# Seven-product FFN blocks: sums of products kept in PSUM half banks that ScalarE fills, with another order of the seven

## The chip, the cores and the metric

The kernel runs on one core of one Trainium2 chip. The metric is the device time of one execution in microseconds (us). The engines are called by the names that the profile uses: PE is TensorE (matrix products, with PEld for its weight loads), ACT is ScalarE, DVE is VectorE, POOL is GpSimd and SP is the queue that starts the large loads. PSUM is the memory that TensorE writes its products to; the kernel uses it as eight banks of 128 partitions by 512 fp32 numbers, and a half bank here is 256 of these columns.

## The reference: two layers with a gated FFN each

The reference is a block of two layers on 512 tokens with 1024 features, all in fp32. Each layer has a mixer (a gated linear recurrence in the first, a dilated attention in the second) and then a feed-forward network (FFN), both with a norm before and after and with scales and shifts from a conditioning vector. The change touches the first half of the FFN only, which is this part of the reference:

```python
def swiglu_ffn(u, w_in, w_out):
    gate, up = jnp.split(u @ w_in, 2, axis=-1)
    return (jax.nn.silu(gate) * up) @ w_out
```

`w_in` is 1024 by 5632 (2816 columns for the gate, 2816 for the up half), and `w_out` is 2816 by 1024.

## The kernel before

**Three products for one.** Each fp32 operand is split into a high part, rounded to the shape that TensorE takes at its fast rate (`F32R`), and a low part, the difference. A product is then three matmuls that add up in PSUM: high by high, high by low and low by high. ScalarE makes the high parts with a copy, VectorE the low parts with a subtraction.

**The FFN's columns.** The 2816 gate and up columns are cut in 22 pieces of 128 (`NF` = 22). In function `ffn`, the first `PLAIN[l]` pairs of pieces (three in the first layer, two in the second) are computed plainly, with 512 tokens as the moving operand. The other pieces, 16 in the first layer and 18 in the second, go through `seven_products`, one piece to a block, so there are 34 blocks.

**A block of seven products.** A block computes gate and up for 128 columns. It treats the work as a 2 by 2 matrix product: weights (gate and up, by the lower and the upper half of the 1024 features) times activations (the two halves of the features, by the two halves of the tokens). Seven products of sums take the place of eight plain ones. The sums of activations (`t1`, `t2`, `T3`, `T4`) are made once per FFN by `token_sums`; `B11`, `B21` and `B22` are plain quarters of the activations. The sums of weights are made in every block: `sum_a` on GpSimd (one 128x512 addition), `sum_b` and `sum_c` on VectorE. The plain quarters of the weights (`R`) are split by `r_hi` and `r_lo`, the sums (`Sm`) by `s_hi` and `s_lo`, each in two cuts. Each of the seven products is one call of `run`: four pieces of the 512 features by three matmuls, twelve matmuls of 128x256, into one half bank.

**Where the products were put together.** In the kernel before, `runs` writes the seven products into four banks: one product alone in its half, the others in pairs. The banks come from the pool's tags `mm` and `a`, `b` by turns, so that a block and the next one use different banks. All additions of products are done outside TensorE, into a scratch tile `W` in SBUF: `sums_1` and `sums_2` on VectorE with a copy of one half bank by ScalarE ahead of each, one addition on GpSimd in `sums_2`, then `sums_3` on VectorE. ScalarE takes the SiLU of the gate (128x512), and `finish` on VectorE multiplies it by the up half into `mid`.

**What sets the order.** The loop over blocks stands in `tc.manual_schedule(engines=ORDERED)`: TensorE, ScalarE, VectorE and GpSimd execute in the order in which the program states their instructions. The framework adds the waits between engines. While TensorE works on block i, the other engines prepare the weights of block i + 1, finish block i - 1, and ScalarE's `r_hi` starts on block i + 2. `st.fill()`, at the end of `s_lo`, starts the load of a later block's weights on SP when a buffer has become free.

**The shift.** `B11` is read from a place 144 columns further on in the activation tiles `uh` and `ul`. The copies that move it there stand at the head of `seven_products`, and in block 0 the run of `B11` comes third for that reason.

**Afterwards** `ffn` takes the eight banks for the outputs of `w_out` (`y0` from tag `mm`, `y1` from tags `a` and `b`), and splits `mid` piece by piece.

Of the kernel before, what the change touches and what calls it, by code (L numbers as in the profile page):

```python
# [158 lines left out]
def block_kernel(tc, x, c, positions, ada_w, ada_b, norm_g, hgrn_w_in, lower, hgrn_norm_g, hgrn_w_out,  # L159
# [8 lines left out]
    with ExitStack() as ctx:  # L168
# [268 lines left out]
        def three(ps, ah, al, bh, bl, start, stop):  # L437
            pe.matmul(ps, ah, bh, start=start, stop=False)  # L438
            pe.matmul(ps, ah, bl, start=False, stop=False)  # L439
            pe.matmul(ps, al, bh, start=False, stop=stop)  # L440
# [327 lines left out]
                    dve.tensor_sub(tl[:, k], t[k], th[:, k].bitcast(F32))  # L768
            return cut

        def seven_products(fs, mid, sgp, spare, th, tl):


            fs = list(fs)
            quarter = lambda a, k: a[:, k * 512:(k + 1) * 512]
            Q4 = lambda a: a.rearrange("p (s n) -> p s n", s=4)
            u_of = lambda r, c: [(uh[:, r * 4 + k, c * 256:c * 256 + 256], ul[:, r * 4 + k, c * 256:c * 256 + 256]) for k in range(4)]
            t_of = lambda i: [(th[:, i, k], tl[:, i, k]) for k in range(4)]
            B21, B22 = u_of(1, 0), u_of(1, 1)

            for copy, t in ((act.copy, uh), (dve.tensor_copy, ul)):
                for a, b in ((112, 256), (0, 112)):
                    copy(t[:, 0:4, a + 144:b + 144], t[:, 0:4, a:b].bitcast(F32))
            B11 = [(uh[:, k, 144:400], ul[:, k, 144:400]) for k in range(4)]
            t1, T3, T4, t2 = (t_of(i) for i in range(4))

            W = shared.rearrange("p a (b n) -> p (a b) n", b=2)
            H2 = lambda a: a.rearrange("p (a n) -> p a n", a=2)
            ring = []
            raw, g_of = {}, {}  # L790

            def places(i):

                p = i % 2
                if len(ring) <= p:
                    ring.append((spare if p == 0 else st.part_tiles(R0), st.part_tiles(R0)))
                return ring[p]

            def r_hi(i):
                if i < len(fs):  # L800
                    raw[i] = st.whole()
                    act.copy(places(i)[0][0][:, 0:1536], raw[i][:, 512:])

            def r_lo(i):
                hi, lo = places(i)[0]
                dve.tensor_sub(lo[:, 0:1536], raw[i][:, 512:], hi[:, 0:1536].bitcast(F32))  # L806

            def sum_a(i):
                r = Q4(raw[i])
                pool.tensor_add(r[:, 2], r[:, 2], r[:, 0])  # L810

            def sum_b(i):
                r = Q4(raw[i])
                dve.tensor_tensor(r[:, 0:2], r[:, 0:3:2], r[:, 1:2].broadcast_to((P, 2, 512)), op=OP.add)  # L814

            def sum_c(i):
                r = Q4(raw[i])
                dve.tensor_add(r[:, 3], r[:, 3], r[:, 1])

            def s_cut(i, k):  # L820
                src = Q4(raw[i])[:, 1:3] if k == 0 else Q4(raw[i])[:, 0:4:3]
                return [Q4(t)[:, 2 * k:2 * k + 2] for t in places(i)[1]] + [src]

            def s_hi(i, k):
                hi, lo, src = s_cut(i, k)
                act.copy(hi, src)  # L826

            def s_lo(i, k):
                hi, lo, src = s_cut(i, k)
                dve.tensor_sub(lo, src, hi.bitcast(F32))  # L830
                if k == 1:
                    raw.pop(i)
                    st.fill()

            def run(ps, w, o, us):
                for kt in range(4):
                    a = slice(o + kt * P, o + (kt + 1) * P)
                    three(ps, w[0][:, a], w[1][:, a], *us[kt], kt == 0, kt == 3)

            def runs(i):  # L840
                R, Sm = places(i)
                b = [bank("mm") for _ in range(4)] if i % 2 == 0 else [bank(t) for t in "abab"]
                g_of[i] = b
                half = lambda n, k: b[n][:, k * 256:k * 256 + 256]
                first = [(half(0, 0), R, 0, B11), (half(3, 1), R, 512, T4), (half(1, 0), R, 1024, B21)]
                for k in (1, 2, 0) if i == 0 else range(3):
                    run(*first[k])
                run(half(1, 1), Sm, 0, t2)
                run(half(2, 1), Sm, 1024, T3)
                run(half(2, 0), Sm, 512, t1)  # L850
                run(half(3, 0), Sm, 1536, B22)

            def sums_1(i):

                dve.tensor_tensor(W[:, 0:5:4], W[:, 2:3].broadcast_to((P, 2, 256)), H2(g_of[i][1]), op=OP.add)

            def sums_2(i):

                dve.tensor_tensor(W[:, 1:6:4], W[:, 4:5].broadcast_to((P, 2, 256)), H2(g_of[i][2]), op=OP.add)
                pool.tensor_add(W[:, 3], W[:, 3], W[:, 5])  # L860

            def sums_3(i):

                if i >= 0:
                    dve.tensor_tensor(W[:, 1:3], W[:, 1:6:4], H2(g_of.pop(i)[3]), op=OP.add)
                    act.activation(W[:, 0:2], W[:, 0:2], AF.Silu)

            def finish(i):
                if i >= 0:
                    dve.scalar_tensor_tensor(H2(mid(fs[i])), W[:, 2:4], -1.0, W[:, 0:2], op0=OP.mult, op1=OP.mult)  # L870

            with tc.manual_schedule(engines=ORDERED):
                r_hi(0)
                r_lo(0)
                sum_a(0)
                sum_b(0)
                sum_c(0)
                for k in range(2):
                    s_hi(0, k)
                    s_lo(0, k)  # L880
                r_hi(1)
                for i in range(len(fs)):
                    more = i + 1 < len(fs)
                    runs(i)
                    sums_3(i - 1)
                    if more:
                        r_lo(i + 1)
                    finish(i - 1)
                    act.copy(W[:, 2], g_of[i][0][:, 0:256])
                    if more:  # L890
                        sum_a(i + 1)
                        sum_b(i + 1)
                        s_hi(i + 1, 0)
                        sum_c(i + 1)
                    sums_1(i)
                    if more:
                        s_lo(i + 1, 0)
                        s_hi(i + 1, 1)
                    act.copy(W[:, 3], g_of[i][2][:, 0:256])
                    if more:  # L900
                        s_lo(i + 1, 1)
                        r_hi(i + 2)
                    sums_2(i)
                sums_3(len(fs) - 1)
                finish(len(fs) - 1)

        def ffn(l, first, close, nxt, side):
            turns.close()
            close()
            with ExitStack() as fx:  # L910
# [4 lines left out]
                with ExitStack() as qx:  # L915
                    sgp = qx.enter_context(tc.tile_pool(name=f"sg{l}", bufs=1, side=side))
                    qp = qx.enter_context(tc.tile_pool(name=f"quarters{l}", bufs=1, side=bass.opposite_side(side)))
                    spare = [qp.tile([P, 3 * 512 + R0 - k * R0], F32R, name=f"spare{l}{k}")[:, R0 - k * R0:] for k in range(2)]
                    qp.tile([P, 112], F32, name=f"pad_q{l}")
                    th = qp.tile([P, 4, 4, 256], F32R, name=f"th{l}")  # L920
                    tl = qp.tile([P, 4, 4, 256], F32R, name=f"tl{l}")
                    for j in range(PLAIN[l]):
                        if j == 0:
                            pss = first
                        else:
                            pss = []
                            for i in range(2):
                                w = st.take()
                                pss += [block(*w, k * P, 256) for k in range(2)]
                        sg = [fresh(sgp, [P, S], "sg", 2) for _ in range(2)]  # L930
                        for k in range(2):
                            act.activation(sg[k], pss[k], AF.Silu)
                        if j == 0:
                            cut = token_sums(th, tl, midt[:, NF - 8:])
                        for k in range(2):
                            dve.tensor_mul(mid(2 * j + k), pss[2 + k], sg[k])
                        if j == 0:
                            cut()
                            fixed.close()
                    seven_products(range(2 * PLAIN[l], NF), mid, sgp, spare, th, tl)  # L940
                fl.drain()
                roll = fx.enter_context(tc.tile_pool(name=f"roll{l}", bufs=1, side=bass.opposite_side(side)))
                y0 = [bank("mm") for _ in range(NT)]
# [969 lines left out]
```

## Time and profile before

| | |
|---|---|
| median of 3 runs | 1515.11 us (1514.31 to 1516.73) |
| span of the profiled execution | 1511.0 us |
| time of the profiled execution itself | not recorded beside its span |
| PE busy | 1492.8 us, 99% of the span |
| DVE, ACT, POOL busy | 70%, 48%, 16% of the span |
| mean granted clock of TensorE | 0.997 |
| blocks of seven products, first FFN | from 381.63 to 535.35 us of the span |
| blocks of seven products, second FFN | from 1211.69 to 1384.61 us of the span |

The span runs from the first to the last instruction; the time of a run has what lies around the span as well. A row of the timeline gives the start in us from the span's start, the duration in us, the engine, the line of the kernel, the operation, what it writes and reads, the shape, and in brackets how long the engine had been idle and what ended the wait. Matmuls overlap, so the spacing of their starts says how fast they go, and not their duration. In the rows of the seven products, `hiq`, `loq` and `spare` are split weights, `uh` and `ul` the activations, `th` and `tl` the sums of activations, `shared` is the scratch tile `W`. A row of the windows gives, for a stretch, its length and the busy time and count of each engine, then the granted clock, the share of the DMA engines and GB/s. A row of the waits gives who waited for whom, the us in total, the times, and the longest.

### The profile page before, as it was taken

How to read it: one execution, taken by the hardware profiler on the slowest of the kernel's cores; microseconds unless marked ns; L12 is line 12 of the kernel's file. 1: busy time of each engine (PE TensorE's matmuls, PEld its weight loads, DVE VectorE, ACT ScalarE, POOL GpSimd, SP SyncE). 2: the span in 40 equal slices, each digit the busy share in tenths (PEclk: the TensorE clock that was granted, in tenths of full speed). 3: DMA queues.
4: the chain of work that ended last, by engine and by line, in shares of the span. 5: the costliest groups of instructions: out<-in, count | busy, mean ns of one | idle time of the engine just before them, and what ended most of it. 6: DMA issues, size and time to landing. Idle time of an engine off the chain costs nothing. (4 is left out here: it accounts for less than half of the span.)

```text
span 1511.0 us, 23542 instructions
## 1 busy us (share of the span) xinstructions
PE 1492.8 (99%) x9231; PEld 1308.2 (87%) x9231; DVE 1063.6 (70%) x1841; ACT 720.3 (48%) x1219; POOL 234.4 (16%) x208
## 2 busy tenths in 40 slices
PE   8999999999999999999999999999999999999998
PEld 6777888898999988888987888988888899999886
DVE  4587867486888896476667766686466978888633
ACT  4433443363454533375545666346655644544231
POOL 1011211031222211140001110011002212221100
PEclk9999999999999999999999999999999999999999
DMA  9654444125333366423166540365213333334521
GB/s 309 183 166 138 156 140 167 56 85 167 113 107 106 105 208 220 155 100 123 57 195 169 150 129 29 113 195 140 84 46 123 98 100 112 109 105 154 209 96 56
DMA packets 206943, 199.14 MB, mean 132 GB/s; under 512 B 6840, under 2 KB 164720, under 8 KB 206576
## 3 DMA queue, kind: packets, MB, share of 16 engines
q1 hardware_dynamic: 203856, 190.87, 40.6%
q10 hardware_dynamic: 1952, 6.65, 1.2%
q8 instruction: 72, 1.18, 0.3%
q0 software_dynamic: 1024, 0.13, 0.2%
q14 instruction: 39, 0.32, 0.1%
HBM read 192.31 MB, written 5.31 MB: 131 GB/s over the span
## 5 line engine op out<-in xcount | busy, mean ns | idle before, releaser
L89 DVE TENSOR_TENSOR lo<-raw,hi 128x2048 fp32r<-128x2048 f32 x68 | 158.8, 2337 | 91.7 <-ACT hi L88 91.7
L88 ACT CAST hi<-raw 128x2048 fp32r<-128x2048 f32 x68 | 129.7, 1908 | 190.3 <-DMA raw<-in_ffn_w_out_dram 55.2
L438 PE MATMUL ps_mm<-apart,hi 128*128 128x512 f32 x384 | 151.4, 394 | 0.0
L439 PE MATMUL ps_mm<-apart,hi 128*128 128x512 f32 x384 | 151.1, 394 | 0.0
L440 PE MATMUL ps_mm<-apart,lo 128*128 128x512 f32 x384 | 150.7, 394 | 0.1
L438 PE MATMUL ps_mm<-uh,hi 128*128 128x512 f32 (+1 forms) x400 | 146.3, 366 | 0.0
L439 PE MATMUL ps_mm<-ul,hi 128*128 128x512 f32 (+1 forms) x400 | 144.3, 361 | 1.0 <-DVE ul L538 1.0
L440 PE MATMUL ps_mm<-uh,lo 128*128 128x512 f32 (+1 forms) x400 | 144.6, 361 | 0.0
L826 ACT CAST hiq<-raw 128x1024 fp32r<-128x1024 f32 x68 | 68.1, 1048 | 64.2 <-DVE raw L814 63.4
L438 PE MATMUL ps_mm<-hi,oh 128*128 128x512 f32 x240 | 94.0, 392 | 0.0
L439 PE MATMUL ps_mm<-lo,oh 128*128 128x512 f32 x240 | 93.4, 389 | 0.0
L438 PEld LDWEIGHTS ps_mm<-uh,hi 128*128 128x128 f32 x400 | 75.5, 189 | 19.7 <-issue 8.4
L439 PEld LDWEIGHTS ps_mm<-ul,hi 128*128 128x128 f32 x400 | 75.6, 189 | 12.1 <-DVE ul L538 1.4
L440 PEld LDWEIGHTS ps_mm<-uh,lo 128*128 128x128 f32 x400 | 75.5, 189 | 11.4
L440 PEld LDWEIGHTS ps_mm<-apart,lo 128*128 128x128 f32 x384 | 72.2, 188 | 15.0 <-DVE lo L89 0.5
L439 PEld LDWEIGHTS ps_mm<-apart,hi 128*128 128x128 f32 x384 | 72.2, 188 | 14.2
L438 PEld LDWEIGHTS ps_mm<-apart,hi 128*128 128x128 f32 x384 | 72.2, 188 | 14.0
L830 DVE TENSOR_TENSOR loq<-raw,hiq 128x1024 fp32r<-128x1024 f32 x68 | 80.0, 1218 | 0.4 <-ACT hiq L826 0.4
L259 DVE SCALAR_TENSOR_TENSOR shared<-raw,cond,shared 128x512 f32<-128x512 f32 x98 | 73.3, 748 | 9.8 <-DMA raw<-in_ada_w_dram 8.8
L261 POOL PARTITION_ALL_REDUCE shared<-shared x14 | 45.9, 3278 | 200.5 <-DVE shared L259 200.5
L810 POOL TENSOR_TENSOR raw<-raw 128x512 f32<-128x512 f32 x34 | 54.7, 1609 | 101.1 <-DVE loq L806 46.3
L440 PE MATMUL ps_mm<-hi,ol 128*128 128x512 f32 x176 | 68.5, 389 | 0.0
(450 smaller groups left out, 4355.2 us busy)
## 6 DMA issues: line engine op xcount, KB each, us to landing
raw<-in_ada_w_dram SPq DMA_DIRECT2D x40, 1024.0 KB, 5.1
raw<-in_ffn_w_in_dram SPq DMA_DIRECT2D x136, 256.0 KB, 3.5
raw<-in_attn_w_in_dram SPq DMA_DIRECT2D x48, 512.0 KB, 5.1
raw<-in_ffn_w_out_dram SPq DMA_DIRECT2D x22, 1024.0 KB, 4.8
raw<-in_hgrn_w_in_dram SPq DMA_DIRECT2D x12, 1024.0 KB, 5.4
raw<-in_attn_w_in_dram SPq DMA_DIRECT2D x12, 1024.0 KB, 4.9
raw<-in_ffn_w_in_dram SPq DMA_DIRECT2D x10, 1024.0 KB, 5.0
first<-in_ada_w_dram SPq DMA_DIRECT2D x14, 512.0 KB, 7.5
```

Of the source, the lines that this page charges most:

```text
L88: self.nc.scalar.copy(hi, t)
L89: self.nc.vector.tensor_sub(lo, t, hi.bitcast(F32))
L259: dve.scalar_tensor_tensor(a, r[:, k], sc, a, op0=OP.mult, op1=OP.add)
L261: pool.partition_all_reduce(a, a, P, bass.bass_isa.ReduceOp.add)
L438: pe.matmul(ps, ah, bh, start=start, stop=False)
L439: pe.matmul(ps, ah, bl, start=False, stop=False)
L440: pe.matmul(ps, al, bh, start=False, stop=stop)
L810: pool.tensor_add(r[:, 2], r[:, 2], r[:, 0])
L826: act.copy(hi, src)
L830: dve.tensor_sub(lo, src, hi.bitcast(F32))
```

## The change

Sums of products are no longer put together by VectorE and GpSimd. They are built in PSUM: ScalarE copies a finished partial sum into another half bank, and the next product is added onto it by matmuls that don't begin afresh (`start=False`).

- The class `Sums` names the half banks of a block: `first` and `both` in two banks taken once per FFN (`fresh_1`, `fresh_x`), `pair` (a bank with halves `u2` and `u4`) and `last` in three banks of the plain part (`pss`, now `seeded`). Blocks alternate between two halves, and between two banks for `pair`.
- The order of the seven is now B11, T3, t2, B21, t1, T4, B22. Before it was B11, T4, B21, t2, T3, t1, B22, with T4, B21, B11 ahead in block 0.
- B11 starts `first`, and T3 starts `both`. ScalarE copies `first` to `u2`; t2 is added onto `u2`, and B21 onto `first`. ScalarE copies `u2` to `last`; t1 is added onto `last`, and T4 onto `u2`. ScalarE copies `last` to `u4`; B22 is added onto `last`. A fourth copy takes `both` to the scratch tile.
- The SiLU is taken in two halves, from `first` and from `last` directly. One VectorE addition (`tail_b`) adds the copy of `both` to the two halves of `pair`, and `tail_c` multiplies, as `finish` did, now ahead of `r_lo` in VectorE's order.
- `sum_a`, `sum_b` and the casts of the next block's weights have other places in the order, both `s_hi` now ahead of the copy to `u4`; the shift copies stand in block 0, after its third copy, and block 0's B11 reads the unshifted quarter.

```diff
+            fresh_1, fresh_x = bank("a"), bank("b")
+            class Sums:
+                def __init__(self, i):
+                    p = i % 2
+                    self.first = half(fresh_1, p)
+                    self.both = half(fresh_x, p)
+                    self.pair = seeded[p]
+                    self.u2, self.u4 = half(self.pair, 0), half(self.pair, 1)
+                    self.last = half(seeded[2], p)
...
+            def run(ps, w, o, us, begin):
                 for kt in range(4):
                     a = slice(o + kt * P, o + (kt + 1) * P)
-                    three(ps, w[0][:, a], w[1][:, a], *us[kt], kt == 0, kt == 3)
+                    for m, (x, y) in enumerate(((0, 0), (0, 1), (1, 0))):
+                        pe.matmul(ps, w[x][:, a], us[kt][y], start=begin and kt + m == 0, stop=kt == 3 and m == 2,
+                                  skip_group_check=True)
...
+            def tail_a(i, s):
+                    act.activation(W[:, 1], s.last, AF.Silu)
+            def tail_b(i, s):
+                    dve.tensor_tensor(W[:, 2:4], W[:, 4 + i % 2:5 + i % 2].broadcast_to((P, 2, 256)), H2(s.pair), op=OP.add)
...
                 for i in range(len(fs)):
                     more = i + 1 < len(fs)
-                    runs(i)
-                    sums_3(i - 1)
+                    R, Sm = places(i)
+                    s = Sums(i)
+                    run(s.first, R, 0, B11[i > 0], True)
+                    run(s.both, Sm, 1024, T3, True)
+                    tail_a(i - 1, before)
+                    tail_b(i - 1, before)
+                    act.copy(s.u2, s.first)
+                    tail_c(i - 1)
+                    run(s.u2, Sm, 0, t2, False)
+                    run(s.first, R, 1024, B21, False)
                     if more:
                         r_lo(i + 1)
-                    finish(i - 1)
-                    act.copy(W[:, 2], g_of[i][0][:, 0:256])
+                        sum_a(i + 1)
+                    act.copy(W[:, 4 + i % 2], s.both)
+                    act.copy(s.last, s.u2)
+                    if i == 0:
+                        shift()
+                    run(s.last, Sm, 512, t1, False)
+                    run(s.u2, R, 512, T4, False)
                     if more:
-                        sum_a(i + 1)
                         sum_b(i + 1)
                         s_hi(i + 1, 0)
                         sum_c(i + 1)
-                    sums_1(i)
-                    if more:
+                        s_hi(i + 1, 1)
                         s_lo(i + 1, 0)
-                        s_hi(i + 1, 1)
-                    act.copy(W[:, 3], g_of[i][2][:, 0:256])
+                    act.copy(s.u4, s.last)
+                    act.activation(W[:, 0], s.first, AF.Silu)
+                    run(s.last, Sm, 1536, B22, False)
                     if more:
                         s_lo(i + 1, 1)
                         r_hi(i + 2)
-                    sums_2(i)
+                    before = s
```

More of the change, by code (lines that the diff above doesn't have):

```diff
@@ L769, in token_sums, with seven_products @@
             return cut
-        def seven_products(fs, mid, sgp, spare, th, tl):
+        def seven_products(fs, mid, seeded, spare, th, tl):
             fs = list(fs)
-            quarter = lambda a, k: a[:, k * 512:(k + 1) * 512]
             Q4 = lambda a: a.rearrange("p (s n) -> p s n", s=4)
@@ L779, in seven_products, with shift @@
             B21, B22 = u_of(1, 0), u_of(1, 1)
-            for copy, t in ((act.copy, uh), (dve.tensor_copy, ul)):
+            B11 = [u_of(0, 0), [(uh[:, k, 144:400], ul[:, k, 144:400]) for k in range(4)]]
+            def shift():
                 for a, b in ((112, 256), (0, 112)):
-                    copy(t[:, 0:4, a + 144:b + 144], t[:, 0:4, a:b].bitcast(F32))
-            B11 = [(uh[:, k, 144:400], ul[:, k, 144:400]) for k in range(4)]
+                    for copy, t in ((act.copy, uh), (dve.tensor_copy, ul)):
+                        copy(t[:, 0:4, a + 144:b + 144], t[:, 0:4, a:b].bitcast(F32))
             t1, T3, T4, t2 = (t_of(i) for i in range(4))
@@ L788, in seven_products @@
             H2 = lambda a: a.rearrange("p (a n) -> p a n", a=2)
+            half = lambda b, k: b[:, k * 256:k * 256 + 256]
             ring = []
-            raw, g_of = {}, {}
+            raw = {}
+            fresh_1, fresh_x = bank("a"), bank("b")
[7 more added lines that the diff above has]
+                    self.last = half(seeded[2], p)
             def places(i):
@@ L833, in s_lo, with tail_c @@
                     st.fill()
-            def run(ps, w, o, us):
+            def run(ps, w, o, us, begin):
                 for kt in range(4):
                     a = slice(o + kt * P, o + (kt + 1) * P)
-                    three(ps, w[0][:, a], w[1][:, a], *us[kt], kt == 0, kt == 3)
[L840 to L862, printed above, removed]
-                if i >= 0:
-                    dve.tensor_tensor(W[:, 1:3], W[:, 1:6:4], H2(g_of.pop(i)[3]), op=OP.add)
-                    act.activation(W[:, 0:2], W[:, 0:2], AF.Silu)
-            def finish(i):
+                    for m, (x, y) in enumerate(((0, 0), (0, 1), (1, 0))):
+                        pe.matmul(ps, w[x][:, a], us[kt][y], start=begin and kt + m == 0, stop=kt == 3 and m == 2,
+                                  skip_group_check=True)
+            def tail_a(i, s):
+                if i >= 0:
+                    act.activation(W[:, 1], s.last, AF.Silu)
+            def tail_b(i, s):
+                if i >= 0:
+                    dve.tensor_tensor(W[:, 2:4], W[:, 4 + i % 2:5 + i % 2].broadcast_to((P, 2, 256)), H2(s.pair), op=OP.add)
+            def tail_c(i):
                 if i >= 0:
@@ L881, in seven_products @@
                 r_hi(1)
+                before = None
                 for i in range(len(fs)):
                     more = i + 1 < len(fs)
-                    runs(i)
-                    sums_3(i - 1)
+                    R, Sm = places(i)
[8 more added lines that the diff above has]
+                    run(s.first, R, 1024, B21, False)
                     if more:
                         r_lo(i + 1)
-                    finish(i - 1)
-                    act.copy(W[:, 2], g_of[i][0][:, 0:256])
+                        sum_a(i + 1)
[5 more added lines that the diff above has]
+                    run(s.u2, R, 512, T4, False)
                     if more:
-                        sum_a(i + 1)
                         sum_b(i + 1)
@@ L902, in seven_products @@
                         r_hi(i + 2)
-                    sums_2(i)
-                sums_3(len(fs) - 1)
-                finish(len(fs) - 1)
+                    before = s
+                tail_a(len(fs) - 1, before)
+                tail_b(len(fs) - 1, before)
+                tail_c(len(fs) - 1)
         def ffn(l, first, close, nxt, side):
@@ L939, in ffn @@
                             fixed.close()
-                    seven_products(range(2 * PLAIN[l], NF), mid, sgp, spare, th, tl)
+                    seven_products(range(2 * PLAIN[l], NF), mid, pss, spare, th, tl)
                 fl.drain()
```

## The prediction

> **What bounds the kernel now.** I read the page's busy table first, then the waits of TensorE, then the two stretches that the change touches as windows, then one block there in order of time.
>
> ```profile
> span 1511.0 us, 23542 instructions
> PE 1492.8 (99%) x9231; PEld 1308.2 (87%) x9231; DVE 1063.6 (70%) x1841; ACT 720.3 (48%) x1219; POOL 234.4 (16%) x208
> ```
>
> TensorE is busy for 99% of the span; no other engine is above 70%. A busy TensorE row may hide a slow one, so the waits come next: eleven rows, the longest and the shortest shown.
>
> ```profile
> PE ps_mm L1140 <- DVE late L1135: 2.0, 3, 1.3
> ...
> PE ps_b L1831 <- ACT h L1809: 1.7, 2, 1.3
> ...
> PE ps_a L1755 <- DVE h L1811: 0.2, 1, 0.2
> ```
>
> None of the eleven is in the seven products; they stand in the mixers and norms. The two windows are blocks 2 to 15 of the first FFN (14 blocks) and all 18 of the second:
>
> ```profile
> core 0: us, PE busy (x) PEld busy (x) DVE busy (x) ACT busy (x) POOL busy (x), PEclk, DMA share, GB/s
> 400.95:535.35 134.40, 134.40 (x1178) 134.40 (x1177) 115.36 (x128) 65.11 (x84) 31.51 (x28) 1.00 0.40 118
> 1211.69:1384.61 172.92, 172.92 (x1513) 172.92 (x1512) 144.41 (x158) 82.64 (x106) 38.52 (x33) 1.00 0.38 111
> ```
>
> Busy equals length in both: TensorE never pauses, at full clock (1.00). 134.40/14 = 9.60 us a block, 84 matmuls. So time here goes up by whatever pause is added, and goes down only if a matmul gets shorter or goes away. One block, first matmuls of B11, T4, the last of t1, the first of B22, the first of the next block:
>
> ```profile
> 448.95 0.28 PE L438 MATMUL ps_a<-uh,hiq 128*128 128x256 f32 x1
> ...
> 450.37 0.29 PE L438 MATMUL ps_b<-th,hiq 128*128 128x256 f32 x1
> ...
> 457.08 0.28 PE L440 MATMUL ps_a<-th,loq 128*128 128x256 f32 x1
> 457.19 0.28 PE L438 MATMUL ps_b<-uh,hiq 128*128 128x256 f32 x1
> ...
> 458.55 0.28 PE L438 MATMUL ps_mm<-uh,spare 128*128 128x256 f32 x1
> ```
>
> A run of twelve matmuls takes 458.55-457.19 = 1.36 us (0.113 each); B11's takes 1.42. What the other engines do beside it:
>
> ```profile
> 450.31 0.63 ACT L866 ACTIVATE shared<-shared 128x512 f32<-128x512 f32 x1 [0.77 <-DVE shared L865]
> 454.93 2.00 ACT L826 CAST hiq<-raw 128x1024 fp32r<-128x1024 f32 x2 [1.97 <-DVE raw L814]
> 457.39 0.37 ACT L899 COPY shared<-ps_a 128x256 f32<-128x256 f32 x1 [0.46 <-PE ps_a L440]
> 457.66 1.48 ACT L802 CAST hiq<-raw 128x1536 fp32r<-128x1536 f32 x1
> ...
> 450.14 1.75 DVE L806 TENSOR_TENSOR spare<-raw,spare 128x1536 fp32r<-128x1536 f32 x1
> 451.81 0.68 DVE L870 SCALAR_TENSOR_TENSOR mid<-shared 128x512 f32<-128x512 f32 x1
> 453.67 1.23 DVE L814 TENSOR_TENSOR raw<-raw 128x1024 f32<-128x1024 f32 x1 [1.18 <-POOL raw L810]
> 455.54 0.68 DVE L855 TENSOR_TENSOR shared<-shared,ps_b 128x512 f32<-128x512 f32 x1
> 456.14 2.35 DVE L830 TENSOR_TENSOR loq<-raw,hiq 128x1024 fp32r<-128x1024 f32 x2
> 458.41 0.68 DVE L859 TENSOR_TENSOR shared<-shared,ps_a 128x512 f32<-128x512 f32 x1
> 459.19 0.69 DVE L865 TENSOR_TENSOR shared<-shared,ps_b 128x512 f32<-128x512 f32 x1
> ...
> 452.02 1.61 POOL L810 TENSOR_TENSOR raw<-raw 128x512 f32<-128x512 f32 x1 [1.78 <-DVE spare L806]
> 459.17 0.74 POOL L860 TENSOR_TENSOR shared<-shared 128x256 f32<-128x256 f32 x1 [5.53 <-DVE shared L859]
> ```
>
> **The change, part by part.** *Matmuls.* 34 blocks of 84 matmuls of 128x256, before and after: 0.
>
> *Removed sums.* Per block VectorE loses L855, L859 and L865 (3 x 0.68) and gains one 128x512 sum; GpSimd loses L860 (0.74). TensorE waits for none of them, so this is worth 0. ScalarE loses a 128x512 SiLU and two copies and gains four copies and two half SiLUs, some 1.0 us more on an engine busy 65.11 of 134.40: 0 by load, and what counts is when each copy runs.
>
> *The copies between runs.* A partial sum now goes on only after a copy. From a run's last matmul to the first of a run that needs the copy: the matmul's own 0.28 (457.08 to 457.36), 0.03 to the copy (457.39), the copy 0.37 (L899, the same size out of PSUM), then TensorE's restart, which this place shows:
>
> ```profile
> 824.13 0.58 ACT L1809 COPY h<-ps_a 128x512 f32<-128x512 f32 x1
> 824.76 0.30 PEld L1831 LDWEIGHTS ps_b<-h,V 128*128 128x128 f32 x2 [1.77 <-ACT h L1809]
> 824.76 0.49 PE L1831 MATMUL ps_b<-h,V 128*128 128x128 f32 x2 [1.34 <-ACT h L1809]
> 825.09 0.39 PE L1830 MATMUL ps_b<-h,V 128*128 128x128 f32 x2
> ...
> 825.31 0.39 PE L1831 MATMUL ps_b<-h,V 128*128 128x128 f32 x2
> ```
>
> 0.05 after the copy ended (824.71), and the first pair takes 0.33 against 0.22 for the next: 0.11 more. Sum 0.28+0.03+0.37+0.05+0.11 = 0.84, less the 0.113 that passes anyway: 0.73 us that must lie under another run. A run is 1.36.
> - first to u2: T3's run lies between, 0.63 spare: 0. Its cover gone, 0.73.
> - u2 to last: B21's run lies between: 0.
> - last to u4: T4's run lies between t1 and B22, but T4 accumulates in the other half of the very bank that this copy writes. In the built program the copy waits for 36 matmuls more than the copy into last did: twelve each of B21, t1 and T4. It starts only after T4, the run before B22, and B22 adds onto what the copy read and waits for it. Nothing is left to cover it: 0.73 a block.
>
> The Trainium skill, "PSUM — Partial Sum Buffer", section "PSUM bank collisions raise a hardware error", says that TensorE and ScalarE must not touch one bank and quadrant of partitions together, even at different columns, so waits go by bank and not by address. By that rule the price is the 0.73 above; by address alone the halves are disjoint, and the price would be 0. No run here shows a collision; the wait in the built program agrees with the rule.
>
> The unknown is a copy that writes PSUM; no row does. From below, the slope alone, half of what L1809 takes beyond L899: (0.58-0.37) = 0.21, so 0.57 a block. From above, 0.63, the 128x512 L866: 0.99. I take 0.37, the same size from the same memory. Ends: 34 x 0.57 = 19 us and 34 x 0.99 = 34 us.
>
> *What stands ahead of the u4 copy on ScalarE.* The two L826 casts, which wait for a chain from the block's start: SiLU of the block before (0.20 after its end, some 0.40), L870's product 0.68, L806 1.75, L810 1.61, L814 1.23, the casts 2.00 = 7.87, and five hand-overs of 0.03 to 0.13: about 8.2. T4 ends at 1.42 + 5 x 1.36 = 8.22, and the copy may start 0.20 later: 8.42. The chain is just inside: 0. Behind the waiting copy stand the SiLU of first and the L802 cast; 0.37+0.27+1.48 later they end at about 10.5, when the next block's first SiLU is due (10.33+0.20): 0.
>
> *T3 from fifth to second.* The last weight cast it needs (L830's pair, ended 458.49) was ready before the block began (458.55); now needed 1.42 after a start that itself comes 0.73 later: 0.
>
> *The shift copies*, from before block 0 into it:
>
> ```profile
> 379.67 1.26 ACT L783 CAST uh<-uh 128x576 fp32r<-128x576 f32 x2
> 382.02 1.85 DVE L783 CAST ul<-ul 128x576 fp32r<-128x576 f32 x2
> ```
>
> They were hidden under T4 and B21; now they stand ahead of block 1's weight casts and of block 0's u4 copy, which waits for T4 anyway. 0, at most 1.3 us in each FFN if the casts slip.
>
> *Queues and ends.* The DMA issues keep their order and SP passes nothing new; GpSimd has one instruction fewer in its chain. After the last block the output products use the same banks: the ninth matmul needs the last VectorE sum, which can run under B22. 0, at most 1 us each.
>
> **Sum.** 34 x 0.73 = 24.8 us. The record has the profiled execution as its span, 1511.0, which is 4.1 below the median of 1515.1; the 4.1 around it stays. Span 1535.8, time 1539.9.
>
> **Rivals.**
> 1. *Not slower.* The u4 copy gets under T4's run, as the other two get under theirs. It decides if the copy's start does not depend on T4's end: then 0.63 is spare and TensorE stays gapless. For it: disjoint halves and ScalarE idle half the time. Against: the count in the wait. Price 0: 1515 us, or 1512 if B11's slower 0.06 and T4's 0.02 a block went too (34 x 0.08 = 2.7).
> 2. *All three copies show.* If a copy into PSUM took over 0.37+0.63 = 1.0 us, the first two would stick out as well; at 1.1 us each: 34 x (0.73+0.73+0.10+0.10) = 56, 1571 us. Short of that, one only as long as 0.63 gives 1549. Against: no ScalarE row of this size is above 0.63.
> 3. *A slower clock after each pause.*
>
> ```profile
> 1174.51 1.09 PE L519 MATMUL ps_b<-ident,xn 128*128 128x128 f32 x8 [0.58 <-DVE xn L513]
> ...
> 1175.87 0.28 PE L438 MATMUL ps_mm<-uh,hi 128*128 128x256 f32 x1
> 1175.98 0.28 PE L439 MATMUL ps_mm<-ul,hi 128*128 128x256 f32 x1
> ```
>
> After a pause of 0.58 matmuls come 0.11 apart, so the trace speaks against it. If the run after each pause went at half rate: 34 x 1.36 = 46 more, 1586 us. The Trainium skill, "TensorE: Matmul & The Clock Gate", section "A second HAM failure mode: psum-queue depth-cycling", tells of short idles between groups of matmuls that cost clock; the clock of 1.00 in the windows shows none so far.
>
> **How the numbers follow.** Forecast 0.86; rival 1 0.06; rival 2 with its shorter form 0.06; rival 3 0.02. The forecast's own ends are 1515 + 19 = 1534 and 1515 + 34 = 1549; that range, 1534 to 1549, holds the forecast nearly whole and leaves out about 0.15. A change below 0.2%, 3 us, can't be told from none. Slower 0.94 (forecast, 2, 3), same 0.05 and faster 0.01 (rival 1).
>
> **What would show it.** In the waits of TensorE a new row of 34 pauses, released by ScalarE's copy into u4, of 0.5 to 0.7 each; each pause between T4 and B22 and nowhere else; blocks of 10.3 us; TensorE's busy time unchanged, its share near 97%; copies into PSUM of about 0.37; no waits behind the copies into u2 and last. Wrong would be: no such row; pauses at t2 or t1; matmuls over 0.113 apart after a pause; or a copy that starts later than 0.2 after T4, held by the casts.

## The result, and the profile after

The changed kernel takes 1537.32 us in the median (1535.01 to 1538.07), the kernel before 1514.96 us beside it. The ratio is 1.0144, with a 95% interval of 1.0129 to 1.0158: slower by 1.4%, some 22 us. The execution that was profiled took 1537.67 us itself, with a span of 1536.0.

The page's first lines and busy table of the changed kernel:

```profile
span 1536.0 us, 23393 instructions
PE 1503.7 (98%) x9231; PEld 1312.8 (85%) x9231; DVE 1024.2 (67%) x1773; ACT 745.8 (49%) x1321; POOL 199.4 (13%) x174
```

The same 9231 matmuls, VectorE and GpSimd relieved, and a span 25.0 us longer than the 1511.0 of before. The busy table alone would mislead: TensorE is still at 98%, and its busy time even rose by 10.9 us. The waits of TensorE tell more (who waited for whom, us in total, times, longest):

```profile
PE ps_mm L856 <- ACT ps_mm L909: 15.2, 34, 0.4
PE ps_mm L1153 <- DVE cols L1183: 2.4, 1, 2.4
```

The top row is new: 34 waits, one for each block, all released by L909, ScalarE's copy into `u4`. There is no row for the copies into `u2` (L890) and `last` (L898). One such wait in order of time: the end of T4's run and the start of B22 on TensorE, then the first matmul of the block that these belong to and of the block after it.

```profile
464.53 0.28 PE L856 MATMUL ps_mm<-tl,hiq 128*128 128x256 f32 x1
464.65 0.28 PE L856 MATMUL ps_mm<-th,loq 128*128 128x256 f32 x1
465.37 0.39 PE L856 MATMUL ps_mm<-uh,hiq 128*128 128x256 f32 x1 [0.45 <-ACT ps_mm L909]
465.59 0.28 PE L856 MATMUL ps_mm<-ul,hiq 128*128 128x256 f32 x1
...
456.52 0.28 PE L856 MATMUL ps_a<-uh,hiq 128*128 128x256 f32 x1
...
466.85 0.28 PE L856 MATMUL ps_a<-uh,spare 128*128 128x256 f32 x1
```

The starts of T4's last and B22's first matmul are 465.37-464.65 = 0.72 apart instead of 0.113, and the next follows after 0.22 instead of 0.113. Together 0.71 us more, and the two spacings behind them add 0.01; the block takes 466.85-456.52 = 10.33 instead of 9.60, 0.73 more. Only 0.45 of it is shown as idle, because T4's last matmul counts as busy for its 0.28 and the late first matmul for 0.39. That is why the waits sum to 15.2 us only, and busy time rose though no matmul was added. What ScalarE and GpSimd did in the same block:

```profile
462.30 2.00 ACT L843 CAST hiq<-raw 128x1024 fp32r<-128x1024 f32 x2 [1.01 <-DVE raw L831]
464.96 0.36 ACT L909 COPY ps_mm<-ps_mm 128x256 f32<-128x256 f32 x1 [0.66 <-PE ps_mm L856]
465.23 0.39 ACT L910 ACTIVATE shared<-ps_a 128x256 f32<-128x256 f32 x1
...
459.72 1.29 POOL L827 TENSOR_TENSOR raw<-raw 128x512 f32<-128x512 f32 x1 [9.04 <-DVE spare L823]
```

The copy starts 0.03 after T4's last matmul has ended (464.65+0.28 = 464.93) and B22 starts 0.05 after the copy. ScalarE had been idle for 0.66 before it, waiting for TensorE, so the casts did not set its start. TensorE and ScalarE wait for each other, one behind the other, once a block.

### The profile page after: what moved, and what is told of

Same layout as the page of the kernel before. It is cut to its first block, busy times and chain, and to the rows that moved or that the text cites. A ratio compares the mean times of both kernels' runs of the same rounds, so it can differ in the third digit from the quotient of the medians.

```text
span 1536.0 us, 23393 instructions
## 1 busy us (share of the span) xinstructions
PE 1503.7 (98%) x9231; PEld 1312.8 (85%) x9231; DVE 1024.2 (67%) x1773; ACT 745.8 (49%) x1321; POOL 199.4 (13%) x174
## 5 line engine op out<-in xcount | busy, mean ns | idle before, releaser
L856 PE MATMUL ps_mm<-th,hiq 128*128 128x256 f32 x340 | 93.9, 276 | 0.0
L856 PE MATMUL ps_mm<-tl,hiq 128*128 128x256 f32 x340 | 93.9, 276 | 0.0
L856 PE MATMUL ps_mm<-th,loq 128*128 128x256 f32 x340 | 93.9, 276 | 0.0
L827 POOL TENSOR_TENSOR raw<-raw 128x512 f32<-128x512 f32 x34 | 44.9, 1319 | 329.2 <-DVE spare L823 145.8
```

The costliest lines, as they stand in the source:

```text
L856: pe.matmul(ps, w[x][:, a], us[kt][y], start=begin and kt + m == 0, stop=kt == 3 and m == 2, skip_group_check=True)
```

## The experiments

The theory: the two halves `u2` and `u4` lie in one bank, T4 accumulates into the one, so the program makes the copy into the other wait for T4's end, and nothing covers it. The rivals: a copy into PSUM costs its pause wherever it stands; or the casts ahead of it on ScalarE set its time.

**u4 in a bank of its own.** The changed kernel leaves the fourth plain bank empty; `u4` goes there.

```diff
-self.u2, self.u4 = half(self.pair, 0), half(self.pair, 1)
+self.u2, self.u4 = half(self.pair, 0), half(seeded[3], p)
...
-dve.tensor_tensor(W[:, 2:4], W[:, 4 + i % 2:5 + i % 2].broadcast_to((P, 2, 256)), H2(s.pair), op=OP.add)
+dve.tensor_tensor(W[:, 2], W[:, 4 + i % 2], s.u2, op=OP.add)
+dve.tensor_tensor(W[:, 3], W[:, 4 + i % 2], s.u4, op=OP.add)
```

> Edit: u4 goes from the second half of u2's bank into the fourth plain bank, which the changed kernel leaves empty; VectorE's closing sum becomes two sums of 128x256. The copy into u4 then waits for t1's last matmul instead of T4's, and T4's run (1.36 us) can lie over it; it stays behind both weight casts on ScalarE. Theory (the shared bank makes the pause): the 34 pauses of 0.4 to 0.5 us of TensorE behind the copy L909 go, blocks are 9.60 us again instead of 10.33, the span falls by 25 us to about 1511, the time to about 1513 to 1515. It is tight: in the changed kernel the casts ended 0.66 before T4's end plus 0.3, so the copy can end only just before T4 does; a rest of up to 0.2 a block (7 us) is allowed. Rival (a copy that writes PSUM costs TensorE its pause wherever it stands): blocks stay at 10.33, about 1537. Rival (the casts ahead of the copy set its start, not the bank): the pauses shrink by no more than the 0.66 that the casts have to spare, and what is left is released by the copy again.

Measured: 1511.8 us, 0.9991 of the kernel before (0.9979 to 1.0003). The whole loss is gone. T4's last and B22's first matmul on TensorE, then the casts and the copy into `u4` (here L910) on ScalarE:

```profile
458.34 0.28 PE L856 MATMUL ps_mm<-th,loq 128*128 128x256 f32 x1
458.45 0.28 PE L856 MATMUL ps_mm<-uh,hiq 128*128 128x256 f32 x1
...
455.99 2.00 ACT L843 CAST hiq<-raw 128x1024 fp32r<-128x1024 f32 x2 [1.01 <-DVE raw L831]
457.89 0.37 ACT L910 COPY ps_mm<-ps_mm 128x256 f32<-128x256 f32 x1
```

B22 follows T4 after 0.11. The copy now runs while T4's matmuls are under way, and ends at 458.26, 0.19 before B22 starts. It still stands behind the casts, and starts when they let it: this cover is thin, but it holds. The copies are the same, as many and as long; only the bank differs, and VectorE's closing sum, which is in two parts. That refutes the rival by which a copy into PSUM costs a pause wherever it stands.

**The same, with the copy ahead of the second cast.**

```diff
                         sum_c(i + 1)
+                    act.copy(s.u4, s.last)
+                    if more:
                         s_hi(i + 1, 1)
                         s_lo(i + 1, 0)
-                    act.copy(s.u4, s.last)
```

> Edit: as the kernel with u4 in a bank of its own, and the copy into u4 stands ahead of the second of the two weight casts on ScalarE (1.0 us earlier in the queue). Theory (the shared bank makes the pause): TensorE runs without a pause from block to block as in the kernel before, 9.60 us a block, 84 matmuls at 0.113; time 1513 to 1515, same as before, and not faster, since the matmuls are the same. If the kernel with u4 apart alone still shows pauses, they were the casts' and are gone here. Rival (a copy that writes PSUM costs a pause wherever it stands): about 1537.

Measured: 1513.37 us, 0.9994 (0.9984 to 1.0004), the same as before. No wait of TensorE stands behind any of these copies. In the block from 450.30 on the copy ends at 457.74 and B22 starts at 458.55, 0.81 later instead of 0.19. With 0.6 us more of cover (not the 1.0 of the expectation) nothing more is gained: the thin cover of the kernel above cost nothing. The relief of VectorE and GpSimd gains nothing clear of noise either: with the pause gone, a block takes the 9.60 us of its 84 matmuls again.

**T3's run between T4 and B22.** `u4` stays in the shared bank. This lays T3's run over the copy into `u4` and takes it away from the copy into `u2`. The copy of T3's product moves behind the next block's first SiLU (in `tail_a`).

```diff
                     act.activation(W[:, 1], s.last, AF.Silu)
+                    act.copy(W[:, 4 + i % 2], s.both)
...
                     run(s.first, R, 0, B11[i > 0], True)
-                    run(s.both, Sm, 1024, T3, True)
...
-                    act.copy(W[:, 4 + i % 2], s.both)
                     act.copy(s.last, s.u2)
...
                     act.copy(s.u4, s.last)
                     act.activation(W[:, 0], s.first, AF.Silu)
+                    run(s.both, Sm, 1024, T3, True)
                     run(s.last, Sm, 1536, B22, False)
```

> Edit: u4 stays in u2's bank; T3's run moves from the second place of the block to the place between T4 and B22, and the copy of its sum for the closing sums goes behind the next block's first SiLU. Now T3's run (1.36 us) lies between T4, whose end the copy into u4 waits for, and B22, which needs the copy; but nothing lies any more between B11 and t2, which needs the copy into u2. Theory (a pause is what lacks of 0.84 us under a run): no pause at B22, a new one of the same size at t2 (0.73 a block, 0.4 to 0.5 of it idle), blocks 10.33 us, about 1537 again. Rival (B22 waits for something else than the copy's end, or T3's place itself costs): the pause at B22 stays as well, blocks above 11 us, 1560.

Measured: 1548.86 us (ratio 1.0243, 1.0221 to 1.0265), 12 above the expectation. The waits of TensorE in this kernel:

```profile
PE ps_mm L856 <- ACT ps_mm L890: 16.9, 34, 1.3
```

The pause moved to t2, which waits for the copy into `u2` (L890), as expected. But blocks took 10.61 us (B11 to B11, 436.16 to 446.77). The rest stands before B22: T3's last and B22's first two matmuls, then ScalarE's casts and the copy into `u4` (here L908).

```profile
444.99 0.28 PE L856 MATMUL ps_b<-th,loq 128*128 128x256 f32 x1
445.25 0.38 PE L856 MATMUL ps_mm<-uh,hiq 128*128 128x256 f32 x1
445.48 0.28 PE L856 MATMUL ps_mm<-ul,hiq 128*128 128x256 f32 x1
...
442.93 2.00 ACT L843 CAST hiq<-raw 128x1024 fp32r<-128x1024 f32 x2 [2.66 <-DVE raw L831]
444.83 0.37 ACT L908 COPY ps_mm<-ps_mm 128x256 f32<-128x256 f32 x1
```

B22 is 0.15 late and its first matmul 0.11 longer. T4 had ended at 443.91, but the casts came 1.0 us later in the block than in the changed kernel, since the moved copy of T3's product holds up VectorE's closing sum and all that stands behind it. T4 itself ends 0.66 earlier in the block than in the changed kernel, as T3's 1.36 no longer stands ahead of it and the pause at t2, some 0.70, does. So the 0.66 that ScalarE had to spare was more than used up, and the copy waited 0.9 for the casts. That was a side effect of this edit, not foreseen in the expectation.

**The same, with the copy ahead of the second cast**, by the same edit as above.

> Edit: as the kernel with T3's run between T4 and B22, and the copy into u4 stands ahead of the second of the two weight casts on ScalarE. That kernel took 10.61 us a block and not the 10.33 expected of it: beside the pause at t2 (0.45 idle) its trace shows B22 starting 0.15 late with a first matmul 0.11 longer, 0.05 after a copy that began only when the casts were done (444.83 against T4's end at about 443.9). Theory (T3 covers the copy, and the casts ahead of it in the queue used up the cover): that late start at B22 goes, 0.24 to 0.28 a block, 34 x 0.24 to 0.28 = 8 to 10 us less than the 1548.9 of that kernel, 1539 to 1541, and the pause at t2 stays as it is. Rival (the late start at B22 is T3's or the bank's own): it stays near 1549.

Measured: 1549.92 us (1.0229, 1.0213 to 1.0245). T3's last and B22's first matmul, and the copy into `u4` (here L906):

```profile
446.16 0.28 PE L856 MATMUL ps_b<-th,loq 128*128 128x256 f32 x1
446.28 0.28 PE L856 MATMUL ps_mm<-uh,hiq 128*128 128x256 f32 x1
...
445.07 0.36 ACT L906 COPY ps_mm<-ps_mm 128x256 f32<-128x256 f32 x1
```

The late start is gone: the copy ends at 445.43, 0.85 before B22. The time didn't fall: in its number this is the rival's outcome, but not for the rival's reason. The matmuls on t1, t2 and T4 took longer here. One form of them (the columns are busy us, mean ns of one, idle before), first in this kernel, then in the one with `u4` apart:

```profile
L856 PE MATMUL ps_mm<-tl,hiq 128*128 128x256 f32 x340 | 95.4, 281 | 0.0
```

```profile
L856 PE MATMUL ps_mm<-tl,hiq 128*128 128x256 f32 x340 | 93.9, 276 | 0.0
```

Runs of twelve matmuls took 1.41 us instead of 1.36, in all blocks but three. The block is 9.60, plus 0.73 for the pause at t2, plus 6 x 0.05 for the six runs that were quick before: 10.63, and 10.62 was seen. So what was gained at B22 was lost to pace; the pace is taken up below.

**The copy into u4 twice.**

```diff
                     act.copy(s.u4, s.last)
+                    act.copy(s.u4, s.last)
```

> Edit: the copy into u4 is issued twice, one behind the other; all else as changed. Theory (the whole copy lies open, nothing covers any part of it): each pause grows by one copy, 0.36 less whatever of it the two overlap; 34 x 0.27 to 0.36 = 9 to 12 us more, about 1547 to 1549. Rival (a part of the copy is hidden, and the pause is set by something else that ends at the same time, such as the weight casts of the next block): less than 5 us more, 1537 to 1542.

Measured: 1552.12 us (1.0254, 1.0238 to 1.0269), 14.8 above the changed kernel. Both copies on ScalarE, and B22's first matmul:

```profile
443.69 0.36 ACT L909 COPY ps_mm<-ps_mm 128x256 f32<-128x256 f32 x1 [0.67 <-PE ps_mm L856]
444.08 0.36 ACT L910 COPY ps_mm<-ps_mm 128x256 f32<-128x256 f32 x1
...
444.49 0.39 PE L856 MATMUL ps_mm<-uh,hiq 128*128 128x256 f32 x1 [0.83 <-ACT ps_mm L910]
```

The second copy starts 0.39 after the first: the two didn't overlap, and 0.03 lies between them beside their 0.36. The block took 10.77 instead of 10.33. 0.39 is the copy, 0.04 is B22's run at a longer pace (1.52 against 1.48), and 0.01 is B11's. The copy lies open in full; the rival with a hidden part falls. My upper end, 0.36 a block, was too low by the hand-over between the two and by that pace.

**The copy into u4 cut to 32 columns.** 224 of the 256 columns of that sum are left out.

```diff
-                    act.copy(s.u4, s.last)
+                    act.copy(s.u4[:, 0:32], s.last[:, 0:32])
```

> Edit: of u4 the copy carries only the first 32 of its 256 columns; 224 columns of that sum are left out, the rest of the output's work is as changed. Theory (the whole hand-over lies open: last matmul's tail 0.28, copy, restart): the pause shrinks by the length that the copy loses. L1809 and L899 of before (0.58 for 512 columns, 0.37 for 256) give 0.21 for 256 columns, so 224 columns are worth 0.18 a block; 34 x 0.18 = 6 us, about 1531, and 0.55 of the 0.73 stays, for it is the tail, the restart and the fixed part of a copy. Rival (the pause is mostly the moving of the data): it all but goes, 34 x 0.6 = 20 us, about 1517. Rival (the pause is set by something beside the copy): nothing changes, 1537.

Measured: 1530.81 us (1.0105, 1.0091 to 1.0119), 6.5 below the changed kernel. The answers on the copy's line, in this kernel and in the changed one (ns least/median/most, first and last start):

```profile
L909 ACT COPY ps_mm<-ps_mm x34: 170/170/170, 392.4 to 1402.4; 128x32 f32<-128x32 f32 x34
```

```profile
L909 ACT COPY ps_mm<-ps_mm x34: 357/357/357, 392.7 to 1407.7; 128x256 f32<-128x256 f32 x34
```

An eighth of the columns takes 170 of 357 ns, so 0.187 us less, x 34 = 6.4 us. The blocks took 10.15 instead of 10.33: 0.01 of the gain is lost again in B22's run (1.49 against 1.48). The pause keeps 0.55 of its 0.73, as expected: the matmul's tail, the fixed part of the copy, the two hand-overs and the restart. Making the copy smaller can't save this order.

**An aside: where B11 reads.** B11's run takes 1.42 us before and after the change, every other run 1.36. Here `u4` is apart with its early copy, and B11 reads the unshifted place in every block; the shift copies go.

```diff
-                    run(s.first, R, 0, B11[i > 0], True)
+                    run(s.first, R, 0, B11[0], True)
...
-                    if i == 0:
-                        shift()
```

> An aside. Edit: as the kernel with u4 in a bank of its own and its copy ahead of the second cast, and B11's run reads its products' inputs from where B11 was stored first, in every block, so that the eight copies that shift it (four to an FFN) go. Question: B11's run takes 1.42 us and the two matmuls after it 0.02 more where every other run takes 1.36. If the shifted place of the inputs makes it: 34 x 0.06 to 0.08 = 2.0 to 2.7 us less than the kernel with its copy early (1513.4), about 1511. If it is the place in the block (the start of the weights' DMA or the end of the block's casts): the same 1513.4, and B11 still 1.42. If the first place is the worse one: slower by an amount that no row bounds.

Measured: 1522.01 us (1.0046, 1.0032 to 1.006). All runs took 1.41 to 1.42 us. It is the third case: the kernel that reads the unshifted place is the worse one, and worse for all seven runs and not for B11 alone. To part the two edits, the next one keeps the copies. The shift writes over part of the unshifted place, so from block 1 on B11's product isn't the reference's; the work is the same.

```diff
-                    run(s.first, R, 0, B11[i > 0], True)
+                    run(s.first, R, 0, B11[0], True)
```

> An aside, to part the two edits of the kernel without the shift, which took 1522.0 us and in which every run of every block took 1.41 to 1.42 us (0.1175 a matmul) instead of 1.36 (0.1133). Edit here: u4 in a bank of its own with its copy early, the eight shifting copies stay, but every block's B11 reads the unshifted place, as only block 0 does otherwise. If the place that B11 reads decides the pace of the whole block (block 0 of every kernel, which reads the unshifted place, ran at 0.1175 too): all blocks at 0.1175 again, 84 x 0.0042 = 0.35 a block more than B11 alone at the slow pace gives, 34 x 0.27 = 9 us above the 1513.4 of the kernel that differs by this alone, about 1522. If the missing shift copies or the moved times of block 0 did it: 1513 to 1515.

Measured: 1522.94 us (1.0043, 1.0027 to 1.006). The same stretch in windows, for this kernel and the one that differs from it by the place alone (length, busy time and count of PE, PEld, DVE, ACT and POOL, granted clock, DMA share, GB/s):

```profile
403.00:530.00 127.00, 127.00 (x1081) 127.00 (x1080) 94.91 (x104) 68.43 (x116) 16.72 (x13) 1.00 0.37 109
```

```profile
403.00:530.00 127.00, 127.00 (x1113) 127.00 (x1112) 97.01 (x106) 70.90 (x119) 16.73 (x13) 1.00 0.39 112
```

Both are gapless at a clock of 1.00, and the one gets 1081 matmuls done where the other gets 1113. So between these two kernels the place that B11 reads changes the pace of the whole block: 9.89 us a block, 0.118 a matmul, against 9.60, where all runs but B11's and the start of the next go at 0.113. (The expectation has 0.1175, from 1.41/12.) Nobody waits, and the clock is the same.

The place alone doesn't settle the pace, though. In the kernel with T3's run moved and the copy early, B11 reads the unshifted place in the first block of both FFNs. These are the five runs behind t2 in each, the same 60 matmuls in the same order (the count takes in the neighbours at the edges):

```profile
387.53:394.59 7.06, 7.06 (x62) 7.06 (x61) 2.68 (x3) 5.08 (x8) 0.00 (x0) 1.00 0.01 3
1233.40:1240.19 6.79, 6.79 (x62) 6.79 (x61) 2.57 (x3) 4.98 (x8) 0.00 (x0) 1.00 0.00 0
```

One goes at 0.118, the other at 0.113, after the same pause at t2. And before the change the first block's T4 and B21 went at 0.118 ahead of any B11.

## Why the prediction was right

The forecast was 1539.9 us, slower, for one reason; 1537.32 was measured, for that reason.

- *TensorE is gapless in the blocks, so an added pause adds to the time.* Right. With the pause gone (`u4` apart), time and blocks are those of before, though ScalarE carries the new copies.
- *Copies into u2 and last: 0, covered by T3's and B21's runs.* Right: no wait row. With T3's run moved away, the copy into `u2` cost 0.70 over the runs of B11 and t2; "its cover gone, 0.73" was said.
- *The copy into u4 waits for T4 because of the bank.* Right, and shown by the one edit of the bank. The Trainium skill, "PSUM — Partial Sum Buffer", section "PSUM bank collisions raise a hardware error", has waits go by bank, and the traces agree: the copy starts 0.03 after T4's end with halves of one bank, and under T4's matmuls with two. What an actual collision would do, no run shows.
- *0.73 a block.* 0.73 measured by blocks, 0.71 by the terms. Term by term: tail 0.28, to the copy 0.03, copy 0.357 (0.37 assumed), to the restart 0.05, first matmul 0.11 longer, less 0.113. The assumption that was least supported, that a copy writing PSUM costs what one writing SBUF does, was 0.013 too high. Both ends, 0.57 and 0.99, were far off. (The lower end takes 0.21, the whole of what L1809 takes beyond L899, where its sentence says half.)
- *Casts ahead of the copy: 0, just inside.* Right as to 0. ScalarE had 0.66 to spare and not 0.2: the chain ended 7.8 after the block's start and not 8.2, mostly since GpSimd's sum took 1.29 instead of 1.61 us.
- *Ends and shift copies.* No wait there, but something not foreseen: block 0 of the first FFN took 10.57 (383.99 to 394.56) and not 10.33, as six of its runs go at the longer pace, and it was much the same in the second FFN. Half of that stood in the kernel before as well, where T4 and B21 ran first at that pace and the block took 9.72. So the change added some 0.12 in each FFN. Block 0 in the kernel before as a window, then the first matmuls of blocks 0, 1 and 2 after the change:

```profile
381.63:391.35 9.72, 9.72 (x85) 9.72 (x84) 8.19 (x10) 3.43 (x5) 1.44 (x1) 1.00 0.34 98
```

```profile
383.99 0.28 PE L856 MATMUL ps_a<-uh,spare 128*128 128x256 f32 x1
...
394.56 0.28 PE L856 MATMUL ps_a<-uh,hiq 128*128 128x256 f32 x1
...
404.89 0.28 PE L856 MATMUL ps_a<-uh,spare 128*128 128x256 f32 x1
```

- *The sum.* 24.8 predicted for the span, 25.0 measured between the two profiled executions. The blocks give all of it: 326.6 us before, 351.6 after, which is 34 x 0.73 and twice the 0.12. Outside the blocks both executions took 1184.4.
- *From the span to the time.* I added 4.1 us as lying around the span, the difference between a span and the median of other runs. The runs shown since have 1.7 around the span, in every kernel. The other 2.4 means that the profiled execution of before was a quick one (spans of that kernel went from 1510.7 to 1515.4). So the forecast was the median of before plus 24.8. From median to median the time rose by only 22.4 us, and 24.8 lies just outside the interval, 19.5 to 23.9. The blocks of the two traces cost 25.0, so some 2.4 us less elsewhere are left unexplained; one trace of each kernel doesn't show where. The kernel with `u4` apart, whose blocks take what they took before, points the same way (1511.80 against 1514.08 beside it), but its interval still holds no change. That the 25.0 between the spans meets the 24.8 so closely is luck in part, since one of the two executions was a quick one.
- *The rivals.* "Not slower" would have needed a copy that doesn't depend on T4; the edit that makes it so gives just its price, the time of before. "All three copies show" would have needed a copy of over 1.0 us; it takes 0.357. "A slower clock after each pause": the granted clock stayed at 1.00 in blocks 1 to 15 of the first FFN of the changed kernel, with 15 pauses in it. What the Trainium skill tells of in "TensorE: Matmul & The Clock Gate", section "A second HAM failure mode: psum-queue depth-cycling", did not show with one idle of 0.45 us in every 10.33.

```profile
394.56:549.40 154.84, 148.16 (x1262) 145.21 (x1261) 108.41 (x109) 80.77 (x136) 18.16 (x15) 1.00 0.38 112
```

Of the list of what would show it, two points were off: the pauses read 0.45 and not 0.5 to 0.7, and TensorE's busy time rose by 10.9 us (its share is 98% and not 97%). The profile counts the tail of the matmul before and the long first matmul after a pause as busy, 0.28 and 0.11 of each 0.73; 34 x (0.28-0.113+0.11) = 9.4 us, so the busy time was bound to rise. One sign that was to show the forecast wrong, matmuls over 0.113 apart after a pause, did show, but for three spacings only (0.22, 0.12 and 0.12); 0.11 of that was in the sum as the restart.

## What to carry to other kernels

When TensorE adds onto a half bank that another engine has to fill, look at which bank the run before it writes: with the other half of that same bank, the program made the fill wait for the run and the whole hand-over lay open, here 0.73 us of which the copy itself is only half; with another bank it cost nothing. Read such a pause from the starts of matmuls and not from the idle time, which showed 0.45 of it. And where the bound engine is gapless, work that is taken off the others gains nothing as long as its matmuls stay the same; here the blocks took 9.60 us with and without it.

## What was not expected of the hardware

The pace of matmuls of one shape isn't one number. The same 128x256 matmuls, gapless and at a granted clock of 1.00, went at 0.113 or at 0.118 us each, in stretches that last whole blocks. With B11 read from 144 columns further on, only B11 and the first matmuls after it were at the longer pace; with B11 at the unshifted place in every block, every run of every block was, also those that read and write what they did before (9.5 us between the spans, 1523.2 and 1513.7). But with T3's run moved and the copy early, 31 of the 34 blocks were at 0.118 though all of these but one read the shifted place, and a block with the unshifted place went at 0.113 after its pause. So the place of one run's inputs can change how the runs behind it go, and the pace can change at a pause too, without the place. By which mechanism, and why one way or the other, stays open.
